# Hymba block on one core: group 6's split probabilities may also use the two tiles of raw q and k

## The chip, the cores and the metric

One core of a Trainium2 chip runs one transformer block. The engines are TensorE (PE; its weight loads are PEld), VectorE (DVE), ScalarE (ACT), GpSimd (POOL) and SyncE (SP), whose queue issues nearly all DMAs. The metric is the device time of one execution in microseconds (us); less is better. Every kernel is run several times, and the median counts.

## What is computed

The block has 2048 positions and 1024 features. After an RMSNorm and one combined projection there are four heads of differential attention and eight heads of stick-breaking attention. Both are concatenated, projected by w_out and added to the input; then come another RMSNorm and a SwiGLU. The change lies in the stick-breaking half:

```python
def stick_breaking_attention(q, k, v):
    # A[t,s] = beta_ts * prod_{s<j<t}(1 - beta_tj), s < t.
...
        z = jnp.einsum('bqhd,bkhd->bhqk', qb, k).astype(jnp.float32) * scale
        mask = (k_pos[None, :] < q_pos[:, None])[None, None]
        log_1mb = jnp.where(mask, jax.nn.log_sigmoid(-z), 0.0)
        rem = lax.cumsum(log_1mb, axis=3, reverse=True) - log_1mb
        a = jnp.where(mask, jnp.exp(jax.nn.log_sigmoid(z) + rem), 0.0)
        return jnp.einsum('bhqk,bkhd->bqhd', a.astype(v.dtype), v)
```

## The kernel before, in words

**Groups.** The heads are worked on in eight groups: 0 to 3 are one differential head each, 4 to 7 two stick-breaking heads each. While the attention of one group runs, the projections of the next ones run beside it: `advance` pulls tiles of 128 positions from one stream of projections, so that group 6's attention lies beside the second half of group 6's own projections and the first half of group 7's. Group 7's attention lies beside the rest of its projections and the output projection (`out_proj`), whose weights `load_wo` brings in four quarters.

**Precision.** Factors of products are split in two float16 parts, a high and a low one, and TensorE adds up three products.

**One chunk of stick-breaking attention** (`stage_a`, L602 to L627): for a block of 128 queries, one head and up to 1024 keys, TensorE makes the scores (`sc`, L506; L508 adds the causal mask), ScalarE takes two sigmoids (L618, L619), DVE runs the product down the keys (the scan, L621), and DVE or POOL multiplies (L622). Then `split_t` (L449) does three things with the probabilities: `to16` casts them to float16 in a tile `s16` (on ScalarE, L89), `tt` subtracts to get the low part (on POOL, L98), and a transposing DMA on SP's queue (L460) writes both parts, keys first, to a tile `aT`. The `s16` tile is free for another chunk once that DMA has landed; the `aT` tile once TensorE has multiplied it with v (`pv`, L517), which is `lag` chunks later: 7 in groups 4 and 5, 5 in groups 6 and 7. A group has 48 chunks: blocks 0 to 7 have one for each head (128 to 1024 keys), blocks 8 to 15 two for each head, the far one of the two always of 1024 keys.

**Tiles.** There are SB = 3 tiles `s16` and AB = 6 tiles `aT`. In groups 4 and 5, where the projections beside the attention are those of groups 4 to 6 and need no tiles `raw` (raw q and k of groups 0 to 3) and no tiles `st` (split q and k before their transposition, in groups 0 to 3 and 7), these serve too: `split_t` takes a `raw` tile in place of `s16` where the running number `wide` modulo 5 is 1 or 3 (that is two chunks of five, over two tiles), and an `st` tile in place of `aT` where it is 3 modulo 4. `wide` counts from 1 within a group, so that chunk k, counted from 0, has wide = k + 1. In the profile both kinds of tile appear as `s`, and both kinds of transposed tile as `aT`.

In group 6 the projection of group 7 uses the `st` tiles again, but not the `raw` ones. These are next written by `load_wo(2)` (L219 and L220, after squares in L189), the third quarter of w_out. In group 6 `wide` is None, and so three `s16` and six `aT` tiles are all that it uses.

**Order.** Within an engine, instructions run in the order in which the program was laid out. That order is not written out by hand: the kernel asks for it from a simulated timeline with priorities (`schedule_with_timeline_sim=True`, `PRI`: a chunk's front, `at`, and the projections, `pm`, have their own), and the same planning picks which free tile a chunk gets. `stage_b` ties the products with v behind the latest scores on TensorE.

Of the kernel before, what the change touches and what calls it, by code (L numbers as in the profile page):

```python
# [21 lines left out]
S, D, P = 2048, 1024, 128  # L22
# [8 lines left out]
NG = 8  # L31
# [28 lines left out]
def block(tc, a, out):  # L60
# [3 lines left out]
    with top:  # L64
# [8 lines left out]
        def note(e, ns):  # L73
            load[e] += ns * KW[e]
# [6 lines left out]
        def level():  # L81
            for k in load:
                load[k] = 0.0

        def to16(dst, src, n, engines="ADP", psum=False):
            cost = {"A": 0.84 * n + 110, "D": (1.05 if psum else 0.53) * n + 70, "P": 1.1 * n + 80}
            e = pick(**{k: cost[k] for k in engines})
            if e == "A":
                ACT.copy(dst, src)  # L89
            elif e == "D":  # L90
                DVE.tensor_copy(dst, src)
            else:
                POOL.tensor_scalar(dst, src, 1.0, 0.0, op0=ALU.mult, op1=ALU.add)

        def tt(dst, a_, b_, op, n, engines="DP"):
            cost = {"D": 1.15 * n + 70, "P": 2.45 * n + 80}
            e = pick(**{k: cost[k] for k in engines})
            (DVE if e == "D" else POOL).tensor_tensor(dst, a_, b_, op)  # L98

        def pri(k):  # L100
            def deco(f):
                @functools.wraps(f)
                def g(*args):
                    with tc.high_priority(PRI[k]) if PRI[k] else nullcontext():
                        return f(*args)
                return g
            return deco

        def nm(s):
            uid[0] += 1  # L110
            return f"{s}{uid[0]}"
# [144 lines left out]
        with ExitStack() as ph1:  # L256
# [6 lines left out]
            def z4():  # L263
                return zp.tile([P, 1028], F32, tag="z4", bufs=ZB, name=nm("z4"))
# [64 lines left out]
            def turned(g):  # L329
                return 4 <= g < NG - 1  # L330
# [115 lines left out]
                    yield  # L446

            @pri("spl")
            def split_t(src, n, he="ADP", le="DP", wide=None):  # L449
                if wide is not None and wide % 5 in (1, 3):  # L450
                    s16 = pp.tile([P, 4, 256], F32, tag="raw", name=nm("s16"))[:].rearrange("p t n -> p (t n)").bitcast(F16)
                else:
                    s16 = s16p.tile([P, 2048], F16, tag="s16", bufs=SB, name=nm("s16"))
                to16(s16[:, :n], src, n, he)
                tt(s16[:, n : 2 * n], src, s16[:, :n], ALU.subtract, n, le)
                if wide is not None and wide % 4 == 3:
                    aT = pp.tile([P, 4, 4, 2, 64], F16, tag="st", name=nm("aT"))[:].rearrange("p c t s e -> p (c t) (s e)")
                else:
                    aT = sp.tile([P, 16, P], F16, tag="aT", bufs=AB, name=nm("aT"))
                SP.dma_start_transpose(aT[:, : 2 * n // P, :], s16[:, : 2 * n])  # L460
                return aT
# [36 lines left out]
            def fq(g, i):  # L498
                k = 2 if g == NG - 1 else 4
                return (i % k, k)  # L500

            @pri("sc")
            def score_chunk(G, sc, i, q, m, w, cut=False, turned=False):
                terms = ((m, 0), (2 + m, 0), (m, 1)) if turned else ((2 + m, m), (m, m))
                for o, (a_, b_) in enumerate(terms):
                    last = PE.matmul(sc[:, : 128 * w].rearrange("p (t n) -> p t n", n=P), lhsT=G["q"][i // 4][:, a_, i % 4, :], rhs=G["k"][q][:, b_, 0:w, :], start=o == 0, stop=o == len(terms) - 1)  # L506
                if cut:
                    last = PE.matmul(sc[:, 128 * w - P : 128 * w], lhsT=idb[:], rhs=tri[:], start=False, stop=True, skip_group_check=True)  # L508
                return last.ins

            @pri("pv")
            def pv(G, yp, y0, aT, b, n, o, wd, start, stop):
                nb = n // P
                for j in range(nb):
                    v = G["v"][2 * b + j // 4][:, j % 4, :]
                    for q, (a_, v_) in enumerate(((j, o), (j, o + wd), (nb + j, o))):
                        PE.matmul(yp[:, y0 : y0 + wd], lhsT=aT[:, a_, :], rhs=v[:, v_ : v_ + wd], start=start and j == 0 and q == 0, stop=stop and j == nb - 1 and q == 2, skip_group_check=True)  # L517

            def diff_attn(g, G):
                @pri("at")  # L520
                def probs(i):
# [43 lines left out]
                    for (b, n, z0), (_, _, z1) in zip(*zs):  # L565
                        DVE.scalar_tensor_tensor(z0[:, :n], z1[:, :n], rc[:], z0[:, :n], op0=ALU.mult, op1=ALU.add)
                        note("D", 1.05 * n + 130)
                        aTs.append((b, n, split_t(z0[:, :n], n)))
# [26 lines left out]
            def sb_attn(g, G):  # L595
                last = {}
                front = []
                wide = [0]
                lag = PD + 2 if g < NG - 2 else PD

                @pri("at")
                def stage_a(i, m, b):  # L602
                    L = (i + 1) * 128
                    n = min(1024, L - 1024 * b)
                    be, om = z4(), z4()
                    if b == i // 8:
                        DVE.memset(om[:, n : n + 1], 8192.0)
                    else:
                        DVE.tensor_copy(om[:, n : n + 1], last[m][:, 0:1])
                    last[m] = om  # L610
                    for c in range((n - 1) // 512, -1, -1):
                        lo, hi = 512 * c, min(512 * c + 512, n)
                        w = hi - lo
                        sc = ps.tile([P, 512], F32, tag="sc", bufs=4, name=nm("sc"))
                        front.append(score_chunk(G, sc, i, 2 * b + c, m, w // P, b == i // 8 and hi == n, turned(g)))
                        aside = c == 1 and turned(g)
                        beta = be[:, lo:hi] if aside else sc[:, :w]
                        ACT.activation(om[:, lo:hi], sc[:, :w], AF.Sigmoid, scale=G["nkz"][:])  # L618
                        ACT.activation(beta, sc[:, :w], AF.Sigmoid, scale=G["kz"][:])  # L619
                        ov = om[:, lo:hi][:, ::-1]  # L620
                        DVE.tensor_tensor_scan(ov, ov, sc[:, :w], om[:, hi : hi + 1], op0=ALU.mult, op1=ALU.bypass)  # L621
                        (POOL if aside else DVE).tensor_tensor(be[:, lo:hi], beta, om[:, lo + 1 : hi + 1], ALU.mult)  # L622
                        note("A", 1.7 * w + 400)
                        note("D", 2.1 * w + 150)
                        note("P" if aside else "D", (1.65 if aside else 1.05) * w + 100)
                    wide[0] += 1
                    return n, split_t(be[:, :n], n, "A", "P", wide[0] if g < NG - 2 else None)  # L627

                ypd = {}

                def stage_b(i, m, b, n, aT):
                    with tc.issue_after(front[-1]):
                        stage_c(i, m, b, n, aT)

                def stage_c(i, m, b, n, aT):
                    r, k = fq(g, i)
                    if i // k not in ypd:
                        ypd[i // k] = ps.tile([P, 512], F32, tag="yp", name=nm("yp"))
                    yp = ypd[i // k]
                    pv(G, yp, P * r + 64 * m, aT, b, n, 128 * m, 64, r == 0 and m == 0 and b == i // 8, r == k - 1 and m == 1 and b == 0)  # L640
                    if m == 1 and b == 0 and r == k - 1:
                        finish(g, G, i, k, yp)
                        G["fin"] = i + 1

                pend = []
                done = 0
                for i in range(NT):
                    if i % 4 == 0:
                        level()
                    for b in range(i // 8, -1, -1):  # L650
                        for m in range(2):
                            n, aT = stage_a(i, m, b)
                            pend.append((i, m, b, n, aT))
                            if len(pend) > lag:
                                stage_b(*pend.pop(0))
                            done += n // P + CS
                            yield done / (272 + 48 * CS), (i + 1 if b == 0 and m == 1 else i)
                for u in pend:
                    stage_b(*u)
# [638 lines left out]
```

## Time and profile before

| | |
|---|---|
| runs | 2703.69 us median of 3 (2701.29 to 2709.12) |
| profiled execution | 2702.93 us, span 2701.0 us |
| granted TensorE clock | 0.98 |
| attention of group 4 | about 620 to 768 us of the span |
| group 5 | 768 to 925 |
| group 6 | 925 to 1100 |
| group 7 | 1100 to 1357 |
| DMA share in the three stretches before group 7 | 0.97, 0.95, 0.92 |

The span runs from the first to the last instruction of one profiled execution. A row of busy times tells how long each engine worked in a stretch; a row of waits tells which instruction stood idle until what had ended, how long in all, how often, and the longest. In a row of the timeline the bracket at the end is the idle time of the engine before that instruction and what ended it. An issue of a DMA stands on SP's queue (SPq), and its landing is told by a row of its own.

### The profile page before, as it was taken

The page shows a single profiled execution, that of the slowest core. Times are in us where ns is not written, and L with a number is a line of the kernel's source. Part 1 is how long each engine was busy: PE and PEld are TensorE (multiplying, and loading weights), DVE is VectorE, ACT ScalarE, POOL GpSimd, SP SyncE. Part 2 cuts the span into 40 slices and gives each one's busy share as a digit, 9 for nine tenths or more (in the row PEclk, how much of TensorE's full clock was granted, in tenths as well). Part 3 has the DMA queues.
Part 4 walks back from the last instruction along what each step waited for, and adds up shares of the span by engine and source line. Part 5 has one row for each costly group of instructions (what it writes and reads, how often), then busy time and mean ns, then how long its engine had stood idle before and what let it go on. Part 6 is the DMA issues. An engine that isn't in the chain of part 4 may idle for free. (4 is left out here: it accounts for less than half of the span.)

```text
span 2701.0 us, 50505 instructions
## 1 busy us (share of the span) xinstructions
PE 2508.6 (93%) x19628; PEld 1507.6 (56%) x19628; DVE 1959.8 (73%) x3712; ACT 1344.7 (50%) x2487; POOL 1517.8 (56%) x1097
## 2 busy tenths in 40 slices
PE   7998989899988989889999999999999999999999
PEld 4655656577776776567774444444444444444444
DVE  6898879899989889887866877778685543433434
ACT  4665656567978878765634534435352112111121
POOL 2578767768767767545665755665564332322323
PEclk9999999999999999999999999999999999999999
DMA  6778697768989989997996566565748744635532
GB/s 221 211 163 184 143 200 172 172 145 183 195 175 185 178 166 206 208 205 203 230 317 232 211 232 219 207 239 183 253 171 330 304 159 157 234 132 184 202 110 94
DMA packets 619584, 534.40 MB, mean 198 GB/s; under 512 B 480640, under 2 KB 548224, under 8 KB 609104
## 3 DMA queue, kind: packets, MB, share of 16 engines
q1 hardware_dynamic: 617520, 529.09, 70.1%
q8 instruction: 154, 2.52, 0.4%
q0 software_dynamic: 512, 1.36, 0.2%
q14 instruction: 86, 0.70, 0.1%
q10 hardware_dynamic: 1312, 0.72, 0.1%
HBM read 261.08 MB, written 147.32 MB: 151 GB/s over the span
## 5 line engine op out<-in xcount | busy, mean ns | idle before, releaser
L98 POOL TENSOR_TENSOR s<-z,s 128x1024 f16<-128x1024 f32 (+7 forms) x288 | 471.5, 1646 | 141.8 <-ACT s L89 118.2
L506 PE MATMUL sc<-kT,qT 128*128 128x512 f16 (+3 forms) x1520 | 382.7, 354 | 51.1 <-DVE z L622 18.6
L1104 PE MATMUL pd<-wd,act 128*128 128x512 f16 x1764 | 392.8, 380 | 5.3 <-DVE cu L1038 4.7
L621 DVE TENSOR_TENSOR_SCAN z<-z,sc 128x512 f32<-128x512 f32 (+3 forms) x320 | 352.8, 1112 | 56.5 <-ACT sc L619 34.6
L325 PE MATMUL pj<-w,xt 128*128 128x384 f16 x1920 | 354.6, 333 | 17.1 <-ACT raw L374 5.8
L1004 PEld LDWEIGHTS <-wu 128*128 128x128 f16 x1848 | 181.9, 98 | 224.6 <-issue 12.8
L1004 PEld LDWEIGHTS <-wg 128*128 128x128 f16 x1848 | 181.3, 98 | 222.9 <-issue 9.3
L517 PE MATMUL yp<-v,aT 128*128 128x64 f16 (+1 forms) x4896 | 271.2, 205 | 36.9 <-DMA aT<-s 35.7
L517 PEld LDWEIGHTS <-aT 128*128 128x128 f16 x4896 | 239.1, 100 | 114.4 <-DMA aT<-s 46.7
L98 POOL TENSOR_TENSOR act<-cg,act 128x512 f16<-128x512 f32 x109 | 150.7, 1393 | 259.4 <-ACT act L1063 259.4
L1104 PEld LDWEIGHTS <-act 128*128 128x128 f16 x1764 | 172.9, 98 | 213.5 <-issue 7.2
L325 PEld LDWEIGHTS <-xt 128*128 128x128 f16 x1920 | 187.8, 99 | 147.2 <-issue 23.4
L89 ACT CAST s<-z 128x128 f16<-128x128 f32 (+7 forms) x215 | 173.3, 810 | 135.9 <-DMA aT<-s 44.6
L98 POOL TENSOR_TENSOR stages<-stages 128x512 f32<-128x512 f32 x97 | 171.4, 1767 | 116.5 <-DVE wg L220 42.2
L618 ACT ACTIVATE z<-sc,c 128x512 f32<-128x512 f32 (+3 forms) x320 | 211.2, 665 | 24.4 <-PE sc L506 12.4
L98 POOL TENSOR_TENSOR hs<-hs,cu 128x512 f32<-128x512 f32 x102 | 133.6, 1317 | 159.3 <-DVE hs L1110 59.7
L506 PEld LDWEIGHTS <-qT 128*128 128x128 f16 x1520 | 128.8, 99 | 119.7 <-issue 23.9
L831 PE MATMUL po<-wo,mt 128*128 128x256 f16 x1536 | 182.4, 279 | 12.6 <-DVE xf L834 8.6
L1063 ACT CAST act<-cg 128x512 f16<-128x512 f32 x126 | 76.7, 616 | 231.1 <-DVE cg L1069 192.7
L1110 DVE SCALAR_TENSOR_TENSOR hs<-pd,c,hs 128x512 f32<-128x512 f32 x144 | 106.0, 747 | 115.0 <-PE pd L1104 105.3
L341 PE MATMUL pj<-xt,w 128*128 128x128 f16 x2304 | 177.4, 222 | 6.2 <-DVE v L363 5.2
L1004 PE MATMUL pm<-X,wu 128*128 128x512 f16 x792 | 179.8, 381 | 2.1 <-ACT cg L1049 1.7
(254 smaller groups left out, 4812.3 us busy)
## 6 DMA issues: line engine op xcount, KB each, us to landing
xt<-xs SPq DMA_DIRECT2D x112, 512.0 KB, 4.5
hs<-hd SPq DMA_DIRECT2D x72, 512.0 KB, 4.5
hd<-hs SPq DMA_DIRECT2D x56, 512.0 KB, 5.9
split<-wg SPq DMA_DIRECT2D x11, 1792.0 KB, 6.9
split<-wu SPq DMA_DIRECT2D x11, 1792.0 KB, 6.7
split<-wd SPq DMA_DIRECT2D x11, 1792.0 KB, 6.8
wg<-split SPq DMA_DIRECT2D x11, 1792.0 KB, 7.5
wd<-split SPq DMA_DIRECT2D x11, 1792.0 KB, 9.0
```

Source lines behind the costliest of these rows:

```text
L89: ACT.copy(dst, src)
L98: (DVE if e == "D" else POOL).tensor_tensor(dst, a_, b_, op)
L325: PE.matmul(pj[:, :384], lhsT=xv[:, xi, kt, :], rhs=G["w"][:, wi, kt, :], start=n == 0, stop=n == 23)
L341: PE.matmul(o, lhsT=x_ if c == 2 else w_, rhs=w_ if c == 2 else x_, start=n == 0, stop=n == 23)
L506: last = PE.matmul(sc[:, : 128 * w].rearrange("p (t n) -> p t n", n=P), lhsT=G["q"][i // 4][:, a_, i % 4, :], rhs=G["k"][q][:, b_, 0:w, :] ...
L517: PE.matmul(yp[:, y0 : y0 + wd], lhsT=aT[:, a_, :], rhs=v[:, v_ : v_ + wd], start=start and j == 0 and q == 0, stop=stop and j == nb - 1 a ...
L618: ACT.activation(om[:, lo:hi], sc[:, :w], AF.Sigmoid, scale=G["nkz"][:])
L621: DVE.tensor_tensor_scan(ov, ov, sc[:, :w], om[:, hi : hi + 1], op0=ALU.mult, op1=ALU.bypass)
L831: PE.matmul(po[:, sl], lhsT=mt[:, kt, P * xi : P * xi + P], rhs=wos[2 * h + n][wi][:, kt, :], start=q == 0, stop=q == 23)
L1004: PE.matmul(ps_[:].rearrange("p (t n) -> p t n", n=P), lhsT=wv[:, wo, wi, 128 * kt : 128 * kt + 128], rhs=X[xo][:, :, xi, kt, :], start=st ...
L1104: PE.matmul(po[:], lhsT=act[:, ao, xi, 128 * j : 128 * j + 128], rhs=W["d"][:, wo, wi, :], start=start and u == 0 and q == 0, stop=u == nu ...
L1110: DVE.scalar_tensor_tensor(dst, po[:], kd[:], src, op0=ALU.mult, op1=ALU.add)
```

## The change

`split_t` gets another argument, `at`, which says whether `st` tiles may take the place of `aT`. Group 6 now passes the running number too, with `at` false: two of five of its chunks put their split probabilities in the `raw` tiles, and all of them keep to the six `aT` tiles. The lag in group 6 stays 5, and groups 4, 5 and 7 pass what they passed before.

```diff
-            def split_t(src, n, he="ADP", le="DP", wide=None):
+            def split_t(src, n, he="ADP", le="DP", wide=None, at=True):
                 if wide is not None and wide % 5 in (1, 3):
                     s16 = pp.tile([P, 4, 256], F32, tag="raw", name=nm("s16"))[:].rearrange("p t n -> p (t n)").bitcast(F16)
                 else:
                     s16 = s16p.tile([P, 2048], F16, tag="s16", bufs=SB, name=nm("s16"))
                 to16(s16[:, :n], src, n, he)
                 tt(s16[:, n : 2 * n], src, s16[:, :n], ALU.subtract, n, le)
-                if wide is not None and wide % 4 == 3:
+                if wide is not None and wide % 4 == 3 and at:
...
                     wide[0] += 1
-                    return n, split_t(be[:, :n], n, "A", "P", wide[0] if g < NG - 2 else None)
+                    return n, split_t(be[:, :n], n, "A", "P", wide[0] if g < NG - 1 else None, g < NG - 2)
```

## The prediction

> **What bounds the kernel now.** I read the page's head first, then the busy time of each engine stage by stage, then who waited for whom inside group 6.
>
> ```profile
> span 2701.0 us, 50505 instructions
> ...
> PE 2508.6 (93%) x19628; PEld 1507.6 (56%) x19628; DVE 1959.8 (73%) x3712; ACT 1344.7 (50%) x2487; POOL 1517.8 (56%) x1097
> ```
>
> TensorE is busy for 93% of the span, so only what shortens TensorE's idle time (or puts some in) reaches the end. The next rows are the attention of group 4, group 5 and group 6; columns are the stretch, its length, busy us of PE, PEld, DVE, ACT and POOL, the granted clock, the DMA share and GB/s. The stretches are cut where the casts (L89) of one group's probabilities end and the next group's begin.
>
> ```profile
> 620.00:768.00 148.00, 134.05 (x2087) 107.69 (x2086) 139.16 (x238) 129.82 (x243) 116.27 (x88) 1.00 0.97 187
> 768.00:925.00 157.00, 140.38 (x2199) 113.28 (x2195) 142.48 (x244) 130.80 (x236) 114.48 (x87) 0.99 0.95 183
> 925.00:1100.00 175.00, 154.80 (x2084) 115.90 (x2082) 153.30 (x277) 136.02 (x249) 119.52 (x90) 0.97 0.92 190
> ```
>
> Groups 4 and 5 already run with five tiles of split probabilities and group 6 with three. TensorE's busy share is 134.05/148 = 0.906, 140.38/157 = 0.894 and 154.80/175 = 0.885. Group 6 leaves TensorE 175 - 154.8 = 20.2 us idle, and that is all that the change can win inside it. Its longest waits there, in total, times, longest, are:
>
> ```profile
> PE yp L517 <- DMA aT<-s: 5.2, 5, 2.0
> PE sc L506 <- DVE z L622: 4.2, 7, 1.1
> ```
>
> Neither is a wait for a free tile of split probabilities. That wait is ScalarE's: its cast (L89) into a tile that an earlier transposing DMA still reads. Here are the totals for group 6, group 5, and group 6 with the start of group 7 (925 to 1115).
>
> ```profile
> ACT s L89 <- DMA aT<-s: 7.8, 7, 2.0
> ACT s L89 <- DMA aT<-s: 6.3, 3, 3.0
> ACT s L89 <- DMA aT<-s: 12.0, 11, 2.3
> ```
>
> **The change part by part.** No instruction is added or removed: every cast, subtraction and transposing DMA stays, with the same operands' sizes. What changes is in which of five tiles a chunk of group 6 lands, and so what each cast waits for. By the code chunk k of a group (48 chunks, counted from 0) takes a raw tile when k mod 5 is 0 or 2. Before, the cast of chunk k waits until the transposing DMA of about chunk k-3 has landed; afterwards that of about chunk k-5. The single waits, in order of time (start, duration, and the idle time before it in brackets):
>
> ```profile
> 933.43 0.41 ACT L89 CAST s<-z 128x256 f16<-128x256 f32 x1 [0.98 <-DMA aT<-s]
> 936.62 0.41 ACT L89 CAST s<-z 128x256 f16<-128x256 f32 x1 [1.65 <-DMA aT<-s]
> 941.17 0.51 ACT L89 CAST s<-z 128x384 f16<-128x384 f32 x1 [1.12 <-DMA aT<-s]
> 954.71 0.83 ACT L89 CAST s<-z 128x768 f16<-128x768 f32 x1 [0.39 <-DMA aT<-s]
> 1001.48 1.05 ACT L89 CAST s<-z 128x1024 f16<-128x1024 f32 x1 [1.98 <-DMA aT<-s]
> 1029.27 1.05 ACT L89 CAST s<-z 128x1024 f16<-128x1024 f32 x1 [0.37 <-DMA aT<-s]
> 1044.19 1.04 ACT L89 CAST s<-z 128x1024 f16<-128x1024 f32 x1 [1.30 <-DMA aT<-s]
> 1105.33 0.30 ACT L89 CAST s<-z 128x128 f16<-128x128 f32 x1 [2.26 <-DMA aT<-s]
> ```
>
> *Term 1, inside the group.* The four waits from 954.71 to 1044.19 make 0.39 + 1.98 + 0.37 + 1.30 = 4.04 us, and I expect all four to go: group 5, with five tiles, has its three waits of this kind at its start, of which term 2 shows the two long ones. ScalarE's time isn't TensorE's, though. These are 4 us around the wait of 1.98, the one of 1.30 and the one of 0.37:
>
> ```profile
> 999.50:1003.50 4.00, 4.00 (x54) 4.00 (x53) 3.97 (x7) 1.42 (x2) 2.62 (x3) 0.74 0.80 165
> 1042.50:1046.50 4.00, 3.59 (x56) 2.64 (x55) 3.51 (x8) 2.70 (x6) 2.25 (x2) 1.00 1.12 240
> 1028.50:1032.50 4.00, 3.07 (x54) 2.21 (x52) 3.88 (x7) 3.63 (x9) 2.20 (x4) 1.00 1.08 232
> ```
>
> Over the longest wait TensorE is busy for all of its 4.00 us: matmuls queued ahead hide it. Over the other two it is idle for 0.41 and 0.93 us, of which the second can owe the cast no more than its 0.37. So I take -0.41 - 0.37 = -0.8 us. The ends are 0 and, if every us of ScalarE came through, -4.0.
>
> *Term 2, the start of the group.* Here the change costs. The raw tiles come into group 6 straight from chunks 45 and 47 of group 5, its last two in raw tiles. Group 5 shows what that does, since it inherits them from group 4 in the same way:
>
> ```profile
> 772.65 0.30 ACT L89 CAST s<-z 128x128 f16<-128x128 f32 x1 [2.88 <-DMA aT<-s]
> 780.23 0.40 ACT L89 CAST s<-z 128x256 f16<-128x256 f32 x1 [3.04 <-DMA aT<-s]
> ```
>
> These two make 5.9 of the 6.3 us that group 5 waits in all; by the casts' widths they are its chunk 0 or 1 (128) and 2 or 3 (256). Group 6 has 0.98 + 1.65 + 1.12 = 3.75 at its start. For group 6 I work out the landing from issue and latency, chunk 45 first, then 47:
>
> ```profile
> 923.29 2.16 SPq L460 DMA_TRANSPOSE aT<-s  x1
> DMA to landing us min/median/max: 4.3/4.3/4.3
> 931.37 2.27 SPq L460 DMA_TRANSPOSE aT<-s  x1
> DMA to landing us min/median/max: 4.9/4.9/4.9
> ```
>
> They land at 927.6 and 936.3. Chunk 2's cast then starts 936.3 - 933.43 = 2.8 us later; the waits of 1.65 and 1.12 behind it disappear. Chunk 0 or 1, cast from 925.18 on, can lose up to 927.6 - 925.2 = 2.4 more. ScalarE idles for 0.98 + 2.8 = 3.8 to 6.2 us against 3.75, so 0 to +2.5. Behind the waiting cast on ScalarE stand the sigmoids (L618, L619) of the next chunk, and DVE's scan (L621) waits for them. I take +0.5, nearer to nothing, because the rest is a shift of waits already there.
>
> *Term 3, the start of group 7.* Group 7 keeps its three own tiles, but group 6's chunks 45 and 47 then lie in raw tiles and no longer in these, so the wait of 2.26 at 1105.33 should go, and some of the rest of 12.0 - 7.8 = 4.2 us. Around it, and at TensorE's next stall, the trace has:
>
> ```profile
> 1103.00:1107.00 4.00, 4.00 (x36) 2.51 (x35) 3.87 (x12) 1.62 (x5) 1.92 (x2) 1.00 1.07 156
> 1112.34 0.35 PE L517 MATMUL yp<-v,aT 128*128 128x64 f16 x6 [1.03 <-DMA aT<-s]
> ```
>
> TensorE again doesn't stop at the time of the wait; 5 us later it stalls for a transposed tile for 1.03 us, which casts 2.26 us earlier would cover. I take -1.0; the ends are 0 and -4.2.
>
> *At nothing:* the raw tiles must be free for the third quarter of w_out (load_wo(2)), whose first write to one is this row; the other two are group 6's last transposing DMA.
>
> ```profile
> 1132.96 1.05 ACT L189 ACTIVATE wo<-z 128x1024 bf16<-128x1024 f32 x1
> 1101.78 2.84 SPq L460 DMA_TRANSPOSE aT<-s  x1
> DMA to landing us min/median/max: 5.1/5.1/5.1
> ```
>
> That lands at 1106.9, 26 us before the write. Only if the two came closer than that would the wait be ScalarE's, and then 26 us less whatever it moved.
>
> *The sum:* -0.8 + 0.5 - 1.0 = -1.3 us on the profiled execution, whose time was 2702.93 us (span 2701.0). Its ends are -4.0 - 4.2 = -8.2 and +2.5. The median of the runs shown, 2703.69, is 0.8 above that execution, so I expect a median of about 2702.
>
> The row of landings speaks to one more limit: median time to landing (the middle number) in group 6 with three tiles, then group 5 with five.
>
> ```profile
> DMA to landing us min/median/max: 2.4/4.5/7.9
> DMA to landing us min/median/max: 2.3/4.4/7.8
> ```
>
> More tiles did not lengthen a transfer, nor shorten one. The Trainium skill ("DMA: Bandwidth & Descriptors", Queues, rings and completion order) says that each DMA engine takes the descriptors of a row in ring order. By that rule a cast that is ready sooner only queues sooner behind the same transfers while the engines are near full (share 0.92 in group 6), and the sum would be 0.
>
> **The rivals.** *Faster:* all 12.0 us of ScalarE's waits turn into TensorE's time, because the transposed tiles that TensorE runs short of come sooner: 2702.9 - 12.0 = 2690.9. For it: TensorE's largest wait in the group, 5.2 us, is for such tiles. Against it: TensorE was full over the two longest casts' waits, and even at group 4's share group 6 would take 154.8/0.906 = 170.9, only 4.1 us less. The Trainium skill ("Perfetto Trace Analysis", Optimization Strategy) reads repeated gaps on the engine that should be saturated as a lack of buffers; here the gaps of the kind sit on ScalarE, at 136.02 of 175 us, so by the trace the rule doesn't reach TensorE.
>
> *Slower:* the program's order is planned from a simulated timeline (the kernel's last lines ask for it), and with two more tiles free the planner can put a cast ahead of the next sigmoids, which it couldn't while no tile was free. ScalarE runs in order, so each such cast delays the scan behind it. Group 6's cast and DVE's waits for sigmoids, then the same waits in group 5:
>
> ```profile
> L89 ACT CAST s<-z 128x1024 f16<-128x1024 f32 (+7 forms) x50 | 40.5, 811 | 22.8 <-DMA aT<-s 7.8 <-DVE z L622 4.6 <-issue 3.7
> DVE z L621 <- ACT z L619: 5.8, 5, 4.0
> DVE z L621 <- ACT sc L619: 5.0, 10, 1.0
> DVE z L621 <- ACT sc L619: 6.2, 6, 2.7
> DVE z L621 <- ACT z L619: 3.9, 2, 3.5
> ```
>
> DVE already waits 15 times; one cast of 0.811 us more ahead of each makes 15 x 0.811 = +12.2 us, or 2715.1. It decides from the point where those waits grow clearly past 10.8 us, since DVE, at 153.30 of 175, has the shortest reserve after TensorE. Against it: group 5, with five tiles, has 10.1 us of them in 8 times, not more.
>
> *Nothing at all:* the planner's order and the landings stay so alike that terms 1 to 3 cancel: 2702.9.
>
> **How the numbers follow.** The forecast (order kept, -1.3) gets 0.46, no effect 0.07, the faster rival 0.20 and the slower one 0.27; the slower one has more than the faster because a new order in a stretch where TensorE, DVE and SP's queue are all close to full has more ways to stall than the 20.2 us of idle time have to vanish. A measurement of this kernel can tell about 0.3% (8.1 us) from no change, so the first two count as the same: 0.53. The range is widened from the forecast's own 2694.7 to 2705.4 to both rivals' times: 2691 to 2715.
>
> **What would show it.** Right: in group 6 after its first ten chunks no cast waits for a transposing DMA; at its start casts wait for 4 to 6 us in all; the 2.26 at the start of group 7 is gone; group 6's TensorE share stays between 0.88 and 0.91. Term 2 is wrong if the start of group 6 shows less than 3.75 us, term 3 if the stall at 1112 stays. The forecast as a whole is wrong if the order of casts and sigmoids on ScalarE differs from before, if DVE's waits for sigmoids leave 10.8 by more than a few us, or if the w_out quarter's first write waits.

## The result, and the profile after

| | before | after |
|---|---|---|
| median of the runs side by side (10 each) | 2702.39 us (2700.21 to 2709.12) | 2711.71 us (2706.80 to 2716.95) |
| ratio | | 1.0031, 95% interval 1.0019 to 1.0043 |
| span of the profiled execution | 2701.0 us | 2709.0 us |

The change costs 9.3 us by the medians and 8.0 us by the two profiled spans. This is the head of the page of the changed kernel, with the busy time of each engine:

```profile
span 2709.0 us, 50521 instructions
...
PE 2504.9 (92%) x19628; PEld 1505.1 (56%) x19628; DVE 1957.1 (72%) x3712; ACT 1344.8 (50%) x2487; POOL 1516.5 (56%) x1097
```

TensorE has no more work than before (2504.9 against 2508.6 us), so the 8 us are idle time or a lower clock. To find them, take the same landmark in both executions: the first time that TensorE, in the feed-forward stage, waits for the gate's activation (L1014). Here is that row of the timeline before, and then after:

```profile
1440.22 2.75 PE L1004 MATMUL pa<-X,wg 128*128 128x512 f16 x12 [1.70 <-ACT cg L1014]
```

```profile
1441.14 2.75 PE L1004 MATMUL pa<-X,wg 128*128 128x512 f16 x12 [1.70 <-ACT cg L1014]
```

Up to there, some 340 us behind the end of group 6, the changed kernel has lost 0.9 us. From there to the end before takes 2701.0 - 1440.2 = 1260.8 us and after 2709.0 - 1441.1 = 1267.9, so 7.1 of the 8.0 us are lost in a part of the program that the diff doesn't touch. Most of that is lost soon. Take a second landmark, TensorE's wait for the squares of a later weight (L937), before and then after:

```profile
1616.48 0.60 PE L945 MATMUL fsc<-sq,ones 128*128 128x256 bf16 x4 [1.95 <-ACT sq L937]
```

```profile
1623.50 0.60 PE L945 MATMUL fsc<-sq,ones 128*128 128x256 bf16 x4 [1.95 <-ACT sq L937]
```

From the one landmark to the other it takes 176.3 us before and 182.4 after, 6.1 more; the last 1.0 us is lost behind. The busy time in four stretches behind the out-projection says where in between; the columns are those of the prediction's table. Before:

```profile
1425.00:1465.00 40.00, 35.18 (x169) 17.87 (x167) 22.57 (x35) 23.50 (x28) 21.63 (x14) 0.96 0.53 190
1465.00:1505.00 40.00, 35.17 (x172) 17.59 (x171) 34.30 (x51) 21.54 (x31) 25.75 (x17) 0.96 0.62 230
1505.00:1545.00 40.00, 38.50 (x184) 17.99 (x183) 38.73 (x51) 21.22 (x26) 27.27 (x16) 1.00 0.61 217
1545.00:1590.00 45.00, 43.04 (x206) 19.99 (x204) 28.25 (x43) 12.39 (x14) 25.48 (x18) 1.00 0.81 282
```

After:

```profile
1425.00:1465.00 40.00, 34.30 (x169) 17.63 (x168) 22.07 (x35) 22.05 (x27) 20.46 (x14) 0.96 0.57 195
1465.00:1505.00 40.00, 31.90 (x156) 16.25 (x154) 31.62 (x41) 17.46 (x26) 22.52 (x16) 0.91 0.54 194
1505.00:1545.00 40.00, 37.67 (x179) 17.44 (x178) 36.14 (x54) 20.96 (x26) 24.82 (x15) 1.00 0.74 253
1545.00:1590.00 45.00, 42.52 (x200) 19.44 (x199) 30.54 (x42) 16.31 (x19) 29.55 (x20) 1.00 0.70 244
```

TensorE's busy time sums to 151.89 before and 146.39 after: 5.5 us more idle, 3.3 of them in the second stretch. There the granted clock is lower too, 0.91 against 0.96, which over some 33 busy us is another 1.6. Together that is about 7, a rough sum: the first stretch begins 15 us ahead of the landmark, and the clock is shown to 0.01 only.

What happens in that second stretch is read from ScalarE. Beside the first products of the feed-forward stage it has two jobs: the splits of the next weights (L215, `wu` is w_up), and the sums of squares (L225) of the last two blocks of rows that `build_x` still has to normalise (`bx`, j = 3). Before, three splits come first (the first two are one row):

```profile
1476.50 2.19 ACT L215 ACTIVATE wu<-stages,c 128x1024 f16<-128x1024 f32 x2 [0.25 <-DVE c L204]
...
1485.23 1.05 ACT L225 ACTIVATE bx<-bx 128x1024 f32<-128x1024 f32 x1
```

After, a sum of squares stands ahead of the first three of them, and it has to wait for its rows:

```profile
1479.83 1.06 ACT L225 ACTIVATE bx<-bx 128x1024 f32<-128x1024 f32 x1 [3.96 <-DMA bx<-hd]
...
1480.88 2.17 ACT L215 ACTIVATE wu<-stages,c 128x1024 f16<-128x1024 f32 x2
```

ScalarE stands idle for 3.96 us with the splits queued behind. They start at 1480.88 instead of 1476.50, 4.4 us later (3.5 when the landmark's 0.9 is taken off). The scale that they read was ready at about the same time, when DVE's L204 ended, at 1476.42 before and 1476.50 after. TensorE then waits for the rows' transposition (L1178). Before and after:

```profile
1492.63 1.48 PE L1178 MATMUL xtr<-id,bx 128*128 128x128 f32 x8 [3.08 <-DVE bx L228]
```

```profile
1498.77 1.94 PE L1178 MATMUL xtr<-id,bx 128*128 128x128 f32 x8 [7.11 <-DVE bx L228]
```

One stall of 3.08 us became one of 7.11. Nothing here was edited: the same instructions stand in another order, and by the code the order of the whole program comes out of one simulated timeline. Compared instruction by instruction, TensorE, ScalarE and GpSimd run the same order in both traces up to 925 us, another one from there to 1215, the same again up to 1458, another one to 1550, and the same from there to the end.

Back in group 6, these are ScalarE's waits for a tile, DVE's for sigmoids and TensorE's for transposed tiles after the change, from 927 to 1104, and the busy times there:

```profile
ACT s L89 <- DMA aT<-s: 2.5, 3, 1.1
```

```profile
DVE z L621 <- ACT sc L619: 13.2, 11, 3.7
DVE z L621 <- ACT z L619: 6.2, 3, 4.1
```

```profile
PE yp L517 <- DMA aT<-s: 9.6, 6, 2.5
```

```profile
927.00:1104.00 177.00, 155.66 (x2048) 115.62 (x2046) 150.12 (x272) 135.04 (x246) 117.73 (x89) 0.94 0.92 187
```

The casts' waits shrank from 7.8 to 2.5 us, as meant. DVE's waits for sigmoids grew from 10.8 to 19.4, TensorE's for transposed tiles from 5.2 to 9.6, and TensorE is idle for 21.3 us of 177, before for 20.2 of 175. The profiles of the experiments below tell how far to trust this (925 to 1102). With group 6 untouched (e4, e8, e10) DVE waits 15.1, 13.4 and 12.6 us for sigmoids, with group 6 as changed (e3, e7, e9, e11) 17.4, 18.1, 20.1 and 15.7. TensorE's waits for transposed tiles are 5.8, 6.9 and 8.0 against 8.5, 6.8, 8.9 and 11.5, so these overlap.

### The profile page after: what moved, and what is told of

Read it like the earlier page. It is cut to its first block, busy times and chain, and to the rows that moved or that the text cites. A ratio compares the mean times of both kernels' runs of the same rounds, so it can differ in the third digit from the quotient of the medians.

```text
span 2709.0 us, 50521 instructions
## 1 busy us (share of the span) xinstructions
PE 2504.9 (92%) x19628; PEld 1505.1 (56%) x19628; DVE 1957.1 (72%) x3712; ACT 1344.8 (50%) x2487; POOL 1516.5 (56%) x1097
```

## The experiments

*Theory A:* the change itself moves nothing; what is lost is lost where the planner puts the last rows' sums of squares ahead of w_up's splits, 370 us behind group 6. *Rivals:* the loss comes with group 6 itself (tiles handed on, waits for sigmoids) and only shows later; or the order at the start of the feed-forward stage is a symptom of something else that is late. All runs were timed in five rounds beside the kernel before, in three sessions: its median was 2703.69 us beside e1 to e4, 2700.24 beside e5 to e8 and 2701.66 beside e9 to e11. Medians of different sessions are therefore compared by their ratios. In kernels with added lines the line numbers are 2 to 4 higher: L217 is L215, L227 is L225, L1181 or L1180 is L1178.

**Which chunks of group 6 use the raw tiles.** Three variants of the one condition in the changed kernel: from chunk 8 on (counted from 0), in the first six, in the last eight.

```diff
-  wide[0] if g < NG - 1 else None
+  wide[0] if g < NG - 2 or (g < NG - 1 and wide[0] > 8) else None     # e1
+  wide[0] if g < NG - 2 or (g < NG - 1 and wide[0] <= 6) else None    # e2
+  wide[0] if g < NG - 2 or (g < NG - 1 and wide[0] > 40) else None    # e6
```

> Group 6 uses the raw tiles only from its ninth chunk on, so nothing changes at its start; the planner's order of the feed-forward stage is, row for row on every engine, that of the kernel before. Theory A (the 9 us are lost at the start of the feed-forward stage, because the planner there puts the sum of squares of two rows (L225) ahead of w_up's splits (L215) on ScalarE, which waits for the rows' DMA): 2698 to 2706, no different from before. Rival B (group 6 itself, its five tiles in the middle of the group, is what costs): 2708 to 2714, like the changed kernel.

> Group 6 uses the raw tiles in its first six chunks alone (three chunks in raw tiles); the planner's order of the feed-forward stage is, row for row, that of the changed kernel. Theory A: 2707 to 2716, as slow as the changed kernel, though only three chunks are touched. Rival B (the middle of group 6): 2699 to 2705. Rival C (the waits at group 6's start, 2 to 3 us at the most by the trace of before): 2703 to 2706, and the start of the feed-forward stage without its stall of 7.1 us.

> Group 6 uses the raw tiles only for four of its last eight chunks. The order of the feed-forward stage is a third one, in which the first sum of squares again stands ahead of w_up's splits on ScalarE. Theory A: 2706 to 2716, with ScalarE's wait of about 4 us for the rows' DMA and TensorE's stall of 6 to 8 us for the transposition. Rival B (the number of chunks in raw tiles counts): 2701 to 2706, as only four of 48 are touched.

Measured: from chunk 8 on 2703.56 us, ratio 0.9998 (0.9987 to 1.0008); the first six 2711.06, 1.0031 (1.0016 to 1.0045); the last eight 2704.94, 1.0019 (1.0006 to 1.0032). So forty chunks with the new choice of tiles cost nothing, and six cost as much as all 48. The last eight missed what theory A expected: their median lies in the range of rival B, and ScalarE's wait is 2.77 us and not about 4. They are slower than the kernel before beside them all the same. What the three differ in behind group 7 is the order. From the landmark to the end all four computing engines run the order of the kernel before, row for row, in e1, and that of the changed kernel in e2; e6 has a third one. On ScalarE, from chunk 8 on, then the first six, then the last eight:

```profile
1474.03 2.19 ACT L215 ACTIVATE wu<-stages,c 128x1024 f16<-128x1024 f32 x2 [0.25 <-DVE c L204]
...
1481.71 1.05 ACT L225 ACTIVATE bx<-bx 128x1024 f32<-128x1024 f32 x1
```

```profile
1483.42 1.06 ACT L225 ACTIVATE bx<-bx 128x1024 f32<-128x1024 f32 x1 [3.95 <-DMA bx<-hd]
...
1484.48 2.17 ACT L215 ACTIVATE wu<-stages,c 128x1024 f16<-128x1024 f32 x2
```

```profile
1477.92 1.06 ACT L225 ACTIVATE bx<-bx 128x1024 f32<-128x1024 f32 x1 [2.77 <-DMA bx<-hd]
...
1478.98 2.18 ACT L215 ACTIVATE wu<-stages,c 128x1024 f16<-128x1024 f32 x2
```

The fast one has the splits first; both slow ones have the sum of squares first, with a wait for its rows. TensorE's stalls for the transposition go with it: 2.49 us, 7.10 and 6.89.

**The order set by hand, both ways.** In the changed kernel the last rows' norm is tied behind w_up's last split on ScalarE by the order of the code (`wsplit` collects the splits); group 6 stays changed. In the kernel before, w_up's last splits are tied behind the first of these sums of squares (`sqs`); group 6 stays as it was.

```diff
 # changed kernel, build_x (e3)
-  for z in (xa, xb): norm_tile(...)
+  with tc.issue_after(wsplit[-1]) if j == 3 else nullcontext():
+      for z in (xa, xb): norm_tile(...)
 # kernel before, main loop (e4)
-  end("u")
   if i == 0: tick(1)
+  with tc.issue_after(sqs[-2]) if i == 0 else nullcontext(): end("u")
```

> The changed kernel with one edge more: on ScalarE the sums of squares of the last four rows (L225) stay behind the last split of the weights of the step before. Everything ahead of the feed-forward stage keeps the changed kernel's order. Theory A: the wait of 4 us of ScalarE and DVE in front of w_up's splits goes, TensorE's wait of 7.1 us for the transposition falls to about 3, and the time is 2701 to 2707. Rival B or C (the cost lies in or around group 6): 2708 to 2715, as before this edge.

> The kernel before, group 6 untouched, with w_up's splits put behind the first of the two sums of squares on ScalarE by an edge. Theory A: slower than before by 4 us or more (2706 to 2718), with ScalarE waiting there for the rows' DMA and TensorE waiting longer for the transposition. Rivals B and C: 2699 to 2705, since group 6 is that of before and the order at the start of the feed-forward stage is worth nothing.

Measured: 2702.69 us, ratio 0.9999 (0.9987 to 1.0010), for the changed kernel with the first sum of squares behind those three splits again; 2707.32, 1.0015 (1.0004 to 1.0026), for the kernel before with it ahead of them. In the first, ScalarE has its splits in time and waits little for the rows, though on SP's queue the load of the rows still stands ahead of that of the next gate's weights, as in the changed kernel:

```profile
1473.13 2.19 ACT L217 ACTIVATE wu<-stages,c 128x1024 f16<-128x1024 f32 x2 [0.71 <-DVE c L204]
...
1476.48 1.06 ACT L227 ACTIVATE bx<-bx 128x1024 f32<-128x1024 f32 x1 [0.55 <-DMA bx<-hd]
```

```profile
1467.66 0.45 SPq L1171 DMA_DIRECT2D bx<-hd  x1
1468.16 1.07 SPq L913 DMA_DIRECT2D stages<-in_w_gate_dram  x1
```

```profile
1490.80 1.62 PE L1181 MATMUL xtr<-id,bx 128*128 128x128 f32 x8 [2.64 <-DVE bx L230]
```

So the order of the loads isn't the cause; the order on the engines is. One tie takes away all that the change costs: its interval doesn't overlap the changed kernel's. The tie moves more than one pair, though. Against the changed kernel 30 of ScalarE's rows and 81 of TensorE's stand at another place, all between 1479 and 1557 us, so what is shown is the order of this stretch, and the one pair only as what sets it. The reverse tie makes the untouched kernel slower, by about half as much: its order isn't the changed kernel's row for row, and the stall falls on other products. Here an expectation failed: ScalarE doesn't wait for the rows at all.

```profile
1485.35 1.05 ACT L227 ACTIVATE bx<-bx 128x1024 f32<-128x1024 f32 x1
```

It waits 3.57 us for the next piece of w_gate instead, which now stands ahead, and w_up's splits start at 1486.40. What the kernels with the slow order share is thus late splits, and not the wait for the rows.

**The tie on DVE alone.** The same tie, but behind w_up's last split on DVE (L220). In its trace it holds back DVE's part of the norm alone: the sums of squares on ScalarE still stand ahead of the splits.

```diff
-  DVE.scalar_tensor_tensor(lo, st, sW[:], hi, ...)
+  wsplit.append(DVE.scalar_tensor_tensor(lo, st, sW[:], hi, ...).ins)   # ACT's splits not collected
```

> The changed kernel with only DVE's part of the last two rows' norm tied behind w_up's last split; the sums of squares on ScalarE may stay ahead of the splits. Theory A by way of ScalarE (the wait for the second load of hd on ScalarE holds the splits): it stays slow, 2706 to 2715 us, ScalarE still waits some 4 us for that load, and TensorE's wait for the transposition is 6 to 9 us. Rival (DVE's own wait ahead of its half of the splits is what holds): back to 2700 to 2706 with TensorE's wait at 2 to 4 us.

Measured: 2708.05 us, 1.0026 (1.0014 to 1.0038), slow as theory A had it. ScalarE waits as before the tie, and DVE's half of the splits waits for ScalarE's (L222 is L220):

```profile
1482.20 1.06 ACT L227 ACTIVATE bx<-bx 128x1024 f32<-128x1024 f32 x1 [3.91 <-DMA bx<-hd]
...
1483.26 2.17 ACT L217 ACTIVATE wu<-stages,c 128x1024 f16<-128x1024 f32 x2
```

```profile
1484.42 1.28 DVE L222 SCALAR_TENSOR_TENSOR wu<-stages,c,wu 128x1024 f16<-128x1024 f32 x1 [3.40 <-ACT wu L217]
```

A miss within it: TensorE's stall for the transposition was expected at 6 to 9 us and is 2.83.

```profile
1495.99 1.94 PE L1181 MATMUL xtr<-id,bx 128*128 128x128 f32 x8 [2.83 <-DVE bx L230]
```

The kernel is slow all the same. The long stall is thus a sign of the late splits and not the price itself; part of the price here is probably the clock (last section).

**Moving the transposition.** If the stall for the transposition were the cost, putting it behind the last product of the gate should recover it, in the changed kernel and in the kernel before, in both with the tie of e3 (which in the kernel before asks for the order that it has).

```diff
+  with tc.issue_after(lastmm[0].ins):      # lastmm: the gate's latest product
       PE.transpose(tr[...], z[...], id32[:])
```

> e3's kernel (the change, sums of squares behind the splits) with TensorE's transpositions of the last rows (L1178) put behind the last product of the gate that runs beside them. If TensorE's remaining stall there of 2.6 to 3.1 us is a matter of order alone, it goes, and the time falls by 2 to 3 us against e3: 2697 to 2702. If the matmuls moved ahead only wait for something else (a PSUM bank, DVE), 2701 to 2705.

> The same edge on TensorE in the kernel before, group 6 with three tiles: 2698 to 2702 if the stall goes, 2701 to 2705 if it is only moved. The distance to e7 is what group 6's five tiles are worth once the feed-forward stage is ordered alike: by the terms of the prediction -1.3 us, within -8.2 and +2.5.

Measured: 2703.84 us, 1.0012 (0.9999 to 1.0025), and 2707.99, 1.0026 (1.0013 to 1.0038): no gain in the one, a loss in the other. TensorE stalls for its next product instead; in the changed kernel, then in the kernel before (L1035 is L1031):

```profile
1490.98 4.15 PE L1008 MATMUL pd<-X,wg 128*128 128x512 f16 x12 [4.52 <-DVE cg L1035]
```

```profile
1493.19 5.28 PE L1008 MATMUL pd<-X,wg 128*128 128x512 f16 x12 [4.81 <-DVE cg L1035]
```

What is late for that product is DVE's part of an earlier one (cg); the stall only changed its place. The kernel before missed both of its expected ranges. The distance between the two, which its expectation takes as the worth of group 6's tiles, is -4.2 us; but of the 5.0 us between their spans 2.0 lie behind the landmark, where the two orders differ, so it doesn't price the tiles.

**A longer lag.** Five tiles and a lag of 6 in group 6, one chunk more between a chunk's probabilities and their product with v.

```diff
-  lag = PD + 2 if g < NG - 2 else PD
+  lag = PD + 2 if g < NG - 2 else PD + (g < NG - 1)
```

> The whole change, and beside it a lag of 6 instead of 5 in group 6. All five tiles are in use throughout group 6, yet the planner's order of the feed-forward stage is, row for row, that of the kernel before, with the sums of squares behind w_up's splits. Theory A: 2699 to 2706. Rival B (five tiles in group 6 cost): 2708 to 2715.

Measured: 2705.57 us, 1.0017 (1.0004 to 1.0030); one of its 12 executions took 11184.89 us, unexplained, and is not in the ratio. From the landmark to the end its order is that of the kernel before, row for row, and that part is fast (1258.1 us, see below). Yet the kernel is slower than before. In its profile the loss lies ahead of the landmark, where single executions vary as much. There the end of the out-projection is short of TensorE work, 73.32 busy us from 1355 to 1437 where the kernel before has 76.66; whether the lag causes this was not tried.

**Spreading the last rows.** The norm and the transposition of the last rows handed out three steps at a time over the next steps of the feed-forward loop, instead of all in its first two: in the changed kernel and in the kernel before. Both edits hold the tie of e3; the expectation of e10 says otherwise and is wrong there.

```diff
-  if i < 2: tick(3 if i == 0 else 16)
+  if i < 7: tick(3 if i == 0 else 0 if i == 1 else 3)
...
-  if i == 0: tick(1)
```

> The changed kernel with the sums of squares tied behind w_up's splits, and the last rows of build_x handed out three steps at a time over the first tiles of the feed-forward stage instead of all at once. Theory A (what is lost stands in the first 40 us of the feed-forward stage, where TensorE waits for the normalised rows' transposition): the rows then come just as they are needed, neither the waits for w_up's splits nor for the transposition pile up, and the median is 2696 to 2702 us, TensorE's largest single wait there under 3 us. Rival (the stage is bound by the amount of DVE's and ScalarE's work in it, whatever its order): 2702 to 2708, with the idle time of TensorE only spread over more waits.

> The same spreading in the kernel before, without the change in group 6 and without the tie. Theory A: the median is as in the run of the changed kernel with the spreading, plus or minus 3 us, that is 2696 to 2705. Rival (spreading lets the order fall out anew and the gain depends on luck): anything from 2700 to 2712, and further than 3 us from that run.

Measured: 2721.20 us, 1.0077 (1.0063 to 1.0091), and 2729.96, 1.0112 (1.0094 to 1.0130). Both expectations failed, theory A's the most; the two lie 8.8 us apart, where theory A had 3 at the most. TensorE's longest wait in the stage, in the changed kernel with the spreading, and what ScalarE does just ahead of it (L1065 is the cast of a product's input):

```profile
1560.92 1.03 PE L1106 MATMUL pd<-wd,act 128*128 128x512 f16 x2 [15.29 <-ACT act L1065]
```

```profile
1560.24 1.66 ACT L1065 CAST act<-cg 128x512 f16<-128x512 f32 x3 [7.32 <-DMA xcd<-b]
```

The casts that TensorE needs (L1065) wait until the last rows have been written to memory (xcd). By the code, `build_x` holds one of the two tiles `act` for these rows (`b16`, L1159), and the casts of the next products go into the other and then into this one: rows that are spread out keep it for longer. Spreading the rows thus adds a wait of its own and says nothing on the price of the late splits. No version beats the kernel before by more than its interval.

**All runs cut at the landmarks.** For each profiled execution: the time of the landmark, the time from it to the second landmark (as in the rows above), and the span less the first landmark's time.

| | group 6 as changed | sum of squares | landmark at | to the second | to the end |
|---|---|---|---|---|---|
| before | no | behind splits | 1440.2 | 176.3 | 1260.8 |
| after | yes | ahead | 1441.1 | 182.4 | 1267.9 |
| from chunk 8 (e1) | in part | behind | 1438.9 | 175.0 | 1257.4 |
| first six (e2) | in part | ahead | 1444.1 | 182.1 | 1271.6 |
| last eight (e6) | in part | ahead | 1439.9 | 181.4 | 1264.9 |
| tie, changed (e3) | yes | behind | 1437.5 | 174.1 | 1263.6 |
| reverse tie, before (e4) | no | ahead | 1439.2 | 180.4 | 1267.3 |
| tie on DVE (e11) | yes | ahead | 1443.6 | 182.0 | 1266.3 |
| lag 6 (e5) | yes, lag 6 | behind | 1445.0 | 174.8 | 1258.1 |
| transposition late, changed (e7) | yes | behind | 1436.6 | 178.6 | 1265.4 |
| transposition late, before (e8) | no | behind | 1439.6 | 180.2 | 1267.4 |
| spread, changed (e9) | yes | spread | 1444.4 | 193.4 | 1279.4 |
| spread, before (e10) | no | spread | 1445.0 | 200.2 | 1290.8 |

Up to the landmark the five executions with group 6 as in the change (after, e3, e7, e9, e11) have a mean of 1440.6 us and the four with group 6 untouched (before, e4, e8, e10) one of 1441.0. The change by itself is worth -0.4 us where single executions lie up to 8 us apart: nothing that can be told, and neither can the -1.3 us of the forecast. From the landmark to the second one, the executions with the first sum of squares behind the three splits (before, e1, e3, e5) take 174.1 to 176.3 us, those with it ahead (after, e2, e4, e6, e11) 180.4 to 182.4: two groups with 4.1 us between them, whatever group 6 does. With the transposition moved as well (e7, e8) it is 178.6 and 180.2, though the splits are in time. To the end of the program the two groups come to 1257.4 to 1263.6 and 1264.9 to 1271.6, less clearly apart, because the part behind the second landmark varies from 1082.4 to 1089.5 us in them without regard to the order.

## Why the prediction was wrong

**The forecast of 2702 (order kept, -1.3 us) was wrong in what it left out.** The step that failed is the one at the head of the change's parts: "What changes is in which of five tiles a chunk of group 6 lands, and so what each cast waits for." That bounded the change to group 6 and the start of group 7. The order of the whole rest of the program is planned in one timeline, and it came out otherwise 370 us later. This term, +7.1 us behind the landmark and 6.1 of them up to the second one, had no line in the sum. Taking it out by a tie brings the kernel to 0.9999 of before, and by the landmark the change proper is worth -0.4 us where the sum had -1.3, which executions as far apart as these can't tell from one another.

**The slower rival had the right kind of cause at the wrong place.** It said that the planner would put something ahead of what is urgent on ScalarE, which runs in order; it named group 6's casts and sigmoids, and priced it at +12.2. Its sign for it showed: DVE's waits for sigmoids left 10.8 us for 19.4, where profiles with group 6 untouched have 15.1 at the most. But TensorE paid little for them by the time of the landmark, which moved by 0.9 us. The measured +9.3 us agree with the rival's price by chance only. The range, which reached to the rival, held the time.

**Term 1 (-0.8): the waits went, their gain didn't show.** The casts of group 6 wait three times only, all in the first ten us. TensorE's share of group 6 is 155.66/177 = 0.879, just under the 0.88 to 0.91 that were said, where before it was 0.885.

**Term 2 (+0.5) had the wrong sign.** The start of group 6 was to wait 4 to 6 us; it waits 0.67 + 1.06 + 0.81 = 2.54 against 3.75 before:

```profile
926.85 0.30 ACT L89 CAST s<-z 128x128 f16<-128x128 f32 x1 [0.67 <-DMA aT<-s]
933.02 0.51 ACT L89 CAST s<-z 128x384 f16<-128x384 f32 x1 [1.06 <-DMA aT<-s]
935.48 0.94 ACT L89 CAST s<-z 128x256 f16<-128x256 f32 x2 [0.81 <-DMA aT<-s]
```

A cast of 384 stands ahead of two of 256, which in the rows of before came first. The prediction held the order fixed and let chunk 2 wait for its raw tile until 936.3; the planner put other casts first.

**Term 3 (-1.0): the stall went and another came.** At the start of group 7 the cast's wait of 2.26 is down to 1.19 and TensorE's stall of 1.03 us for a transposed tile is gone. Its waits from 1100 to 1135, before and then after:

```profile
PE sc L506 <- DVE z L622: 2.7, 2, 2.1
PE sc L506 <- DMA qT<-qT: 2.7, 1, 2.7
PE yp L517 <- DMA aT<-s: 1.0, 1, 1.0
PE osc L182 <- DVE st L363: 0.2, 1, 0.2
```

```profile
PE yp L488 <- DVE y L486: 4.7, 1, 4.7
PE sc L506 <- DVE z L622: 2.2, 1, 2.2
```

They sum to 6.6 and 6.9 us. The step from a stall's absence to a gain was the weak one: another wait, of 4.7 us for DVE (y, L486), stands in the same stretch. Whether the one caused the other was not traced.

**What was put at nothing held.** The first write of the w_out quarter to a raw tile comes without a wait:

```profile
1134.21 1.14 ACT L189 ACTIVATE wo<-z 128x1024 bf16<-128x1024 f32 x1
```

**Left open:** why the planner's timeline turns over at that place. All 48 chunks, the first six and the last eight turn it over, the forty from chunk 8 on and the lag of 6 don't; which of its comparisons decides was not traced. Also open is which of the rows that move with the pair makes the price of 4 to 6 us, since the stall changes its place from run to run.

## What to carry to other kernels

Where a planner lays out the whole program from a simulated timeline, an edit at one place is an edit of every order behind it: price it by the stretches in which a little delay can turn two instructions of an in-order engine over, above all where one of them waits for a DMA and the other feeds the busiest engine, and tie that pair by hand. Before a difference in time is put down to the edited lines, cut both traces at a landmark behind them, and at a second one behind the place you suspect. A wait that vanishes from an engine that isn't the bound is not a gain until TensorE's own idle time shows it.

## What the runs showed of the hardware

A stall of TensorE can cost more than its length, because the granted clock falls with it. These are stretches of 4 us around the stall, before (stall of 3.08 us up to 1492.63; the stretches on either side have 1.00), then in the tie on DVE alone (2.83 up to 1495.99, 1.05 up to 1501.39); the third column from the right is the clock:

```profile
1493.00:1497.00 4.00, 3.68 (x18) 2.48 (x16) 2.57 (x4) 2.03 (x4) 0.00 (x0) 0.57 0.91 293
```

```profile
1493.00:1497.00 4.00, 1.17 (x6) 1.04 (x6) 4.00 (x4) 0.89 (x2) 4.00 (x4) 0.81 0.00 0
1497.00:1501.00 4.00, 3.08 (x14) 2.38 (x13) 4.00 (x4) 0.00 (x0) 2.06 (x1) 0.50 0.42 122
1501.00:1505.00 4.00, 3.60 (x9) 1.31 (x9) 1.03 (x2) 3.26 (x6) 1.24 (x2) 0.50 1.06 411
1505.00:1509.00 4.00, 4.00 (x21) 2.05 (x20) 2.71 (x3) 0.98 (x2) 3.37 (x3) 0.91 0.87 304
```

Busy time times the missing clock, an estimate of what it costs, is 3.68 x 0.43 = 1.6 us before, and 1.17 x 0.19 + 3.08 x 0.50 + 3.60 x 0.50 + 4.00 x 0.09 = 3.9 us with the tie on DVE. The first stalls are of much the same length, and 2.3 us more are lost, which would be a part of how that kernel is slow without a long stall; its second stall of 1.05 may be why. Behind the changed kernel's stall of 7.11 us, with 2.23 and 4.00 busy us at a clock of 0.50 and 0.82 (1497 to 1505), it is only 1.8. The loss doesn't follow the length of the stall.

The time at half clock is 4 x 0.43 / 0.50 = 3.4 us before, 4 x (0.17 + 0.50 + 0.18) / 0.50 = 6.8 in the changed kernel (0.83 in the stretch from 1493) and 4 x (0.19 + 0.50 + 0.50 + 0.09) / 0.50 = 10.2 with the tie on DVE: once, twice and three times 3.4. The Trainium skill ("TensorE: Matmul & The Clock Gate", Part 1: The HAM clock gate) says that the clock falls to half after an idle window of about 3.4 us, and that the windows run freely and don't start with the kernel. The trace agrees with the half (0.50) and with steps of 3.4 us. It differs in the idle time needed: with the tie on DVE, 0.81 over the stretch from 1493 to 1497 means that the clock fell at about 1495.5, some 2.3 us into the stall of 2.83, which as a whole is shorter than such a window.

The other thing not expected is how far single executions of one stretch lie apart: with group 6 as changed, the landmark falls between 1436.6 and 1444.4 us. Much of that has nothing to do with group 6: the last of TensorE's waits for a transposed tile in group 5 ends between 919.4 and 924.5 us in the 13 profiles, 923.1 before, and up to there TensorE, ScalarE and GpSimd run the same order in all of them. A difference of 3 us between two profiles, ahead of the landmark, says nothing.
